# Last quarter of the last MLP product with tokens in the partitions, in a two-layer hybrid decoder

## Chip, cores, metric

The kernel runs on one core of one Trainium2 chip. The metric is the device time of one execution in microseconds (us). The median of several runs is compared; one further execution is recorded by the hardware profiler, and its trace gives the profile.

## What is computed

The reference is a decoder of two layers on x of 512 tokens by 1024 (fp32). Each layer has a mixing part (one projection, window attention, retention, two gated products, an output product) and an MLP; at the end stands one more norm.

```python
def rmsnorm(x, g):
    y = x * rsqrt(mean(x * x, axis=-1) + EPS)
    return y * g

def hybrid_layer(x, ...):
    ...                                   # mixing part: x = x + mixed @ w_out
    h2 = rmsnorm(x, g_mlp)                # (512, 1024)
    x = x + square(relu(h2 @ w_up)) @ w_down   # w_up 1024 x 4096, w_down 4096 x 1024
    return x

for l in range(2):
    x = hybrid_layer(x, ...)
return rmsnorm(x, g_final)
```

The change concerns the last quarter of `@ w_down` in layer 2 (1024 of its 4096 rows), the sum with x, and the final norm with `g_final`.

## The kernel before

**Layout.** Everything is held turned: the model dimension lies in the 128 partitions, as `KD` = 8 chunks, and the 512 tokens lie along the free dimension. `x` is a tile of 128 x 8 x 512. A product for one chunk of 128 output features has the weights as the stationary operand (128 x 128) and the activations as the moving one.

**Three products for one.** Each fp32 factor is kept as a high and a low part in the type fp32r. `products` (L293 to L295) issues three matmuls for each pair: high with high, high with low, low with high, all added up in one bank of PSUM.

**Weights.** They arrive in units of 128 x 1024 numbers (512 KB). `load_until` puts the loads on SP's DMA queue, three units ahead of the splitting; `split_until` makes the high part on ScalarE (L248) and the low part on VectorE (L249). The parts go into three rotating buffers `hi`, `lo`, or, at the very end, into `homes`: tiles of four banks that `slots` hands out (names `r...`), so that they can stay there and be used more than once. `first` shifts the place of some units inside the rotating buffers by `ASIDE` numbers.

**The MLP.** `mlp_sequence` interleaves the two products: pairs of `w_up` chunks (`pair`; the last one is `narrow_pair`, whose products have 256 columns) and, behind each quarter, two chunks at a time of `w_down` (`two_chunks`), added to x by `put_down` (L1146). What comes out of `w_up` is squared, split and kept as `up[q]`, eight pairs of 128 x 512, in `r` tiles or in tiles of the tag `big` (`uhi`, `ulo`; six buffers in all). Layer 2's last quarter is `end(layer, uT)`.

**`end` before.** The 512 tokens are cut into two halves of 256, `Half`. For each half the eight chunks of output features are computed one after the other (the first four side by side in four banks, the rest one by one). `put` adds the bank to x, squares the sum, adds up the squares over the chunks in `acc` and multiplies x by the final gain, which is one column for each chunk. The sum over the partitions is a matmul with ones in fp32 (`sums`, L452). `finish` takes the root, the reciprocal of 128 x 256 numbers (L476), multiplies each chunk (L480) and stores it (L482, L484). `first.finish` runs inside the second half's products, `second.finish` behind the last one. The weights' units stay in place for the second half: the first three in `hi` and `lo`, five in `homes`. The output has the shape (128, 8, 512), and the host turns it.

**PSUM.** `ps_mm` has five banks for products, `ps_aux` three for the rest. The kernel adds products to a bank that ScalarE has written in other places too (`resume`, in `narrow_pair` L1056 and `wide_pair` L1111).

**Order.** The program's text gives the priorities; a scheduler with a timing simulation then fixes each engine's order, and an instruction that is ready may be put ahead of earlier ones that aren't. Each engine works in its order, and a queue's DMAs are issued in theirs.

Of the kernel before, what the change touches and what calls it, by code (L numbers as in the profile page):

```python
# [10 lines left out]
F32 = mybir.dt.float32  # L11
F32R = mybir.dt.float32r
AF = mybir.ActivationFunctionType
ALU = mybir.AluOpType
# [104 lines left out]


@with_exitstack
def decoder(ctx, tc, xT, x_first, w_in, w_a, w_b, w_out, w_up, w_down, tables, decay, band, out):
    nc = tc.nc
    weights = {"w_in": w_in, "w_a": w_a, "w_b": w_b, "w_out": w_out, "w_up": w_up, "w_down": w_down}

# [8 lines left out]
    def f32(ap):  # L134
        return ap.bitcast(F32)

    def temp(name="t"):
        return tmp.tile([P, T], F32, tag="t", name=name)
# [4 lines left out]
    def bank(pool, name):  # L143
        return pool.tile([P, T], F32, tag=pool.name, name=name)
# [1 line left out]

    n_gain, n_sink = (2 * DEPTH + 1) * KD, DEPTH * N_Q
    little_x = const.tile([P, P + KD * T], F32, name="x")  # L150
    gain = little_x[:, P - n_gain : P]
    sink = little_x[:, P - n_gain - n_sink : P - n_gain]
# [71 lines left out]
    def split_until(n):  # L224
        while state["split"] < min(n, len(order)):
            i = state["split"]
            load_until(i + 3)
            paired = order[i][1] == "pair"
            if paired:
                add_part(i)  # L230
            raw = raws[i]
            if homes and i >= len(order) - len(homes):
                home = homes[len(order) - 1 - i]
                hi, lo = (home[:, 2 * a : 2 * a + 2, :].rearrange("p a t -> p (a t)") for a in range(2))
            else:


                first = (ASIDE, ASIDE) if paired or i >= len(order) - 8 else (0, 0)
                if paired and wide(order[i][2]):
                    first = (ASIDE, 0)  # L240
                hi, lo = (
                    wpool.tile([P, UNIT + P], F32R, tag=n, name=n)[:, a : a + UNIT] for n, a in zip(("hi", "lo"), first)
                )
            for at in (LEFT,) if paired and order[i][3] == 3 else halves(i):
                if i == 0 and at.start == 0:
                    nc.vector.tensor_copy(hi[:, at], raw[:, at])
                else:
                    nc.scalar.activation(hi[:, at], raw[:, at], AF.Copy)  # L248
                nc.vector.tensor_tensor(lo[:, at], raw[:, at], f32(hi[:, at]), ALU.subtract)  # L249
            raws.pop(i - 3 if paired else i, None)  # L250
            parts[i] = (hi, lo)
            state["split"] += 1

    def unit(name, layer):
        i = state["next"]
        assert order[i][:2] == (layer, name), (order[i], layer, name)
        state["next"] += 1
        split_until(i + 3)
        return parts.pop(i)
# [27 lines left out]
    def products(ps, pairs, start, stop, resume=False):  # L287


        n = len(pairs)  # L290
        for i, ((ah, al), (bh, bl)) in enumerate(pairs):
            more = {"skip_group_check": True} if resume else {}
            nc.tensor.matmul(ps, ah, bh, start=start and i == 0, stop=False, **more)  # L293
            nc.tensor.matmul(ps, ah, bl, start=False, stop=False, **more)  # L294
            nc.tensor.matmul(ps, al, bh, start=False, stop=stop and i == n - 1, **more)  # L295
# [118 lines left out]


    def end(layer, uT):
        homes.extend(slots.four()[0] for _ in range(5))
        units = []
        H = T // 2
        g_last = 2 * DEPTH * KD  # L420

        def unit_at(i):
            if len(units) == i:
                units.append(unit("w_down", layer))
            return units[i]

        def half_products(ps, i, col, moving, at, start, stop):
            hi, lo = unit_at(i)
            cols = slice(col, col + P)
            products(ps, [((hi[:, cols], lo[:, cols]), tuple(m[:, at] for m in moving))], start, stop)  # L430

        class Half:
            def __init__(self, at):
                self.at = at
                self.acc = tmp.tile([P, T], F32, tag="acc", name="acc", bufs=1)[:, :H]

            def put(self, c, ps):
                xa = x[:, c, self.at]
                nc.vector.tensor_tensor(xa, xa, ps, ALU.add)
                if c == 0:  # L440
                    nc.scalar.activation(self.acc, xa, AF.Square)
                else:
                    sq = temp("sq")[:, :H]
                    nc.scalar.activation(sq, xa, AF.Square)
                    if c < KD - 1:
                        nc.vector.tensor_tensor(self.acc, self.acc, sq, ALU.add)
                    else:
                        self.last = sq
                nc.scalar.activation(xa, xa, AF.Copy, scale=gain[:, g_last + c : g_last + c + 1])

            def sums(self, ps, src, start):
                nc.tensor.matmul(ps, f32(ones), src, start=start, stop=not start)  # L452

            def gemm(self, meanwhile=None):
                banks = [bank(ps_mm, "mm")[:, :H] for _ in range(4)]
                for k in range(KD):
                    for c, ps in enumerate(banks):
                        half_products(ps, k // 2, (k % 2) * T + c * P, uT[k], self.at, k == 0, k == KD - 1)
                    if k == 1 and meanwhile:
                        meanwhile()  # L460
                for c, ps in enumerate(banks):
                    self.put(c, ps)
                for c in range(4, KD):
                    ps = bank(ps_mm, "mm")[:, :H]
                    for k in range(KD):
                        half_products(ps, c, k * P, uT[k], self.at, k == 0, k == KD - 1)
                    if c == KD - 1:
                        self.ssq = bank(ps_aux, "ssq")[:, :H]
                        self.sums(self.ssq, self.acc, True)
                    self.put(c, ps)  # L470

            def finish(self):
                self.sums(self.ssq, self.last, False)
                rstd = tmp.tile([P, T], F32, tag="rstd", name="rstd", bufs=2)[:, :H]
                nc.scalar.activation(rstd, self.ssq, AF.Sqrt, bias=eps, scale=1.0 / D)
                nc.vector.reciprocal(rstd, rstd)  # L476
                for k in range(KD):
                    if k % 2 == 0:
                        o = temp("o").rearrange("p (c t) -> p c t", t=H)
                    nc.vector.tensor_tensor(o[:, k % 2, :], x[:, k, self.at], rstd, ALU.mult)  # L480
                    if k in (0, 1, KD - 2, KD - 1):
                        nc.sync.dma_start(out[:, k, self.at], o[:, k % 2, :])  # L482
                    elif k % 2:
                        nc.sync.dma_start(out[:, k - 1 : k + 1, self.at], o)  # L484

        first = Half(slice(0, H))
        first.gemm()
        second = Half(slice(H, T))
        second.gemm(first.finish)
        second.finish()  # L490


    def layer_body(layer):
# [760 lines left out]
    return units  # L1254


def _down_units(w):
    units = []
    for q in range(4):
        rows = w[q * D : (q + 1) * D]  # L1260
        units += _half_grouped(rows) if q == 3 else _units_twos(rows)
    return units


# [31 lines left out]
def _laid_out(x, g_mix, w_in, sinks, w_a, w_b, w_out, g_mlp, w_up, w_down, g_final):  # L1296
    r = np.arange
    wa_rows = np.concatenate([(4 * g + c) * HEAD_DIM + r(HEAD_DIM) for c in range(4) for g in range(2)])
    rotary, decay, band = _tables()
    gains = np.stack([g for l in range(DEPTH) for g in (g_mix[l], g_mlp[l])] + [g_final])  # L1300
    heads = np.array([4 * g + c for c in range(4) for g in range(2)])
    xT = np.ascontiguousarray(x[0].T.reshape(KD, P, T).transpose(1, 0, 2))
    gains = gains.reshape(-1, P).T
    sinks = np.broadcast_to(sinks[:, heads].reshape(1, -1), (P, DEPTH * N_Q))
    return {
        "xT": xT,
        "x_first": np.concatenate([sinks, gains, xT[:, 0, :]], 1),
        "w_in": _stack(w_in, _w_in_units),
        "w_a": _stack(w_a, lambda w: _units_chunks(w[wa_rows], r(D))),
        "w_b": _stack(w_b, _half_grouped),  # L1310
        "w_out": _stack(w_out, _half_grouped),
        "w_up": _stack(w_up, _up_units),
        "w_down": _stack(w_down, _down_units),
        "tables": rotary,
        "decay": decay,
        "band": band,
    }


# [16 lines left out]
```

## Time and profile before

| | us |
|---|---|
| median of 3 runs | 1500.74 (1500.68 to 1500.89) |
| the profiled execution, its own time | 1500.69 |
| its span in the trace | 1498.8 |
| TensorE busy | 1487.5 |
| VectorE busy | 1066.0 |
| ScalarE busy | 757.9 |

The span reaches from the first to the last instruction in the trace; some 1.9 us of the execution's own time lie around it. In the profile PE is TensorE, PEld its weight loads, DVE is VectorE, ACT is ScalarE, SP is the engine that issues most DMAs (SPq is its queue). A timeline row has the start, the length, the engine, the line, the operation, the result and the operands, and in brackets the idle time before it with what ended it. Matmuls are pipelined: each row's length reaches into the next one. A row of one line or tile gives lengths in ns as least, median and greatest.

### The profile page before, as it was taken

How to read it: one execution, taken by the hardware profiler on the slowest of the kernel's cores; microseconds unless marked ns; L12 is line 12 of the kernel's file. 1: busy time of each engine (PE TensorE's matmuls, PEld its weight loads, DVE VectorE, ACT ScalarE, POOL GpSimd, SP SyncE). 2: the span in 40 equal slices, each digit the busy share in tenths (PEclk: the TensorE clock that was granted, in tenths of full speed). 3: DMA queues.
4: the chain of work that ended last, by engine and by line, in shares of the span. 5: the costliest groups of instructions: out<-in, count | busy, mean ns of one | idle time of the engine just before them, and what ended most of it. 6: DMA issues, size and time to landing. Idle time of an engine off the chain costs nothing.

```text
span 1498.8 us, 19490 instructions
## 1 busy us (share of the span) xinstructions
PE 1487.5 (99%) x7468; PEld 1265.3 (84%) x7468; DVE 1066.0 (71%) x1708; ACT 757.9 (51%) x1207; POOL 2.9 (0%) x13
## 2 busy tenths in 40 slices
PE   9999999999999999999999999999999999999997
PEld 7888888888888888888888888888888888888897
DVE  7877568754697777777678765677448877777774
ACT  6657355632564445544455742555226555454562
POOL 0000000000000000000000000000000000000000
PEclk9999999999999999999999999999999999999999
DMA  6422322244323332324443222222442222343331
GB/s 222 128 91 71 99 84 92 71 126 126 98 73 112 99 111 87 112 85 142 155 132 92 85 85 90 82 90 84 126 124 95 91 93 91 99 127 99 102 110 56
DMA packets 52636, 155.03 MB, mean 103 GB/s; under 512 B 6208, under 2 KB 8384, under 8 KB 52544
## 3 DMA queue, kind: packets, MB, share of 16 engines
q1 hardware_dynamic: 52400, 153.54, 32.5%
q8 instruction: 58, 0.95, 0.3%
q14 instruction: 34, 0.28, 0.1%
q10 hardware_dynamic: 144, 0.26, 0.0%
HBM read 146.96 MB, written 4.19 MB: 101 GB/s over the span
## 4 chain that ended last, share of the span: by engine, by line
PE 99%; ACT 1%; DVE 0%; issue 0%; DVEq 0%
PE mm L293 24%; PE mm L295 24%; PE mm L294 24%; PE mm L1085 9%; PE mm L1086 5%; PE rv L293 2%; PE rv L294 2%; PE rv L295 2%; PE score L664 1%; PE pT L629 1%; PE r L294 1%; PE r L295 1%; PE r L293 1%; PE pv L649 0%; PE pv L650 0%; PE ssq L387 0%
## 5 line engine op out<-in xcount | busy, mean ns | idle before, releaser
L248 ACT ACTIVATE hi<-raw 128x1024 fp32r<-128x1024 f32 (+1 forms) x313 | 315.2, 1013 | 451.7 <-PE mm L294 278.6
L249 DVE TENSOR_TENSOR lo<-raw,hi 128x1024 fp32r<-128x1024 f32 (+1 forms) x314 | 363.8, 1164 | 166.7 <-ACT hi L248 165.6
L294 PE MATMUL mm<-r,hi 128*128 128x512 f32 (+1 forms) x784 | 292.9, 374 | 0.0
L293 PE MATMUL mm<-r,hi 128*128 128x512 f32 (+1 forms) x784 | 291.6, 375 | 1.1 <-ACT mm L1056 1.1
L295 PE MATMUL mm<-r,lo 128*128 128x512 f32 (+1 forms) x784 | 288.4, 374 | 0.0
L293 PE MATMUL mm<-xhl,hi 128*128 128x512 f32 (+1 forms) x744 | 283.1, 383 | 0.0
L294 PE MATMUL mm<-xhl,hi 128*128 128x512 f32 (+1 forms) x744 | 281.8, 381 | 0.0
L295 PE MATMUL mm<-xhl,lo 128*128 128x512 f32 (+1 forms) x744 | 280.8, 381 | 0.0
L293 PEld LDWEIGHTS mm<-r,hi 128*128 128x128 f32 x784 | 146.8, 188 | 27.4 <-ACT mm L1056 1.5
L295 PEld LDWEIGHTS mm<-r,lo 128*128 128x128 f32 x784 | 147.0, 188 | 26.6
L294 PEld LDWEIGHTS mm<-r,hi 128*128 128x128 f32 x784 | 147.2, 188 | 25.4
L293 PEld LDWEIGHTS mm<-xhl,hi 128*128 128x128 f32 x744 | 140.2, 189 | 24.8 <-ACT xhl L303 0.4
L295 PEld LDWEIGHTS mm<-xhl,lo 128*128 128x128 f32 x744 | 139.8, 188 | 25.0
L294 PEld LDWEIGHTS mm<-xhl,hi 128*128 128x128 f32 x744 | 139.9, 188 | 24.5
L1085 PE MATMUL mm<-r,hi 128*128 128x512 f32 x352 | 124.4, 391 | 0.0
L1086 PE MATMUL mm<-r,lo 128*128 128x256 f32 x352 | 97.5, 277 | 0.0
L1085 PE MATMUL mm<-xhl,hi 128*128 128x512 f32 x264 | 93.3, 390 | 0.0
L1085 PEld LDWEIGHTS mm<-r,hi 128*128 128x128 f32 x352 | 66.1, 188 | 14.2 <-ACT mm L1111 0.6
L1086 PE MATMUL mm<-xhl,lo 128*128 128x256 f32 x264 | 73.1, 277 | 0.0
L1086 PEld LDWEIGHTS mm<-r,lo 128*128 128x128 f32 x352 | 66.1, 188 | 1.7
L1146 DVE TENSOR_TENSOR x<-x,mm 128x512 f32<-128x512 f32 x56 | 37.8, 686 | 39.0 <-PE mm L295 39.0
L1085 PEld LDWEIGHTS mm<-xhl,hi 128*128 128x128 f32 x264 | 49.6, 188 | 10.2
(210 smaller groups left out, 2110.5 us busy)
## 6 DMA issues: line engine op xcount, KB each, us to landing
raw<-w_in_in SPq DMA_DIRECT2D x89, 512.0 KB, 3.5
raw<-w_down_in SPq DMA_DIRECT2D x64, 512.0 KB, 3.6
raw<-w_up_in SPq DMA_DIRECT2D x36, 512.0 KB, 3.6
raw<-w_up_in SPq DMA_DIRECT2D x56, 256.0 KB, 2.7
raw<-w_b_in SPq DMA_DIRECT2D x16, 512.0 KB, 3.5
raw<-w_out_in SPq DMA_DIRECT2D x16, 512.0 KB, 3.8
raw<-w_a_in SPq DMA_DIRECT2D x8, 512.0 KB, 3.6
x<-xT_in SPq DMA_DIRECT2D x15, 256.0 KB, 3.9
```

The lines of the kernel that those rows point to most:

```text
L248: nc.scalar.activation(hi[:, at], raw[:, at], AF.Copy)
L249: nc.vector.tensor_tensor(lo[:, at], raw[:, at], f32(hi[:, at]), ALU.subtract)
L293: nc.tensor.matmul(ps, ah, bh, start=start and i == 0, stop=False, **more)
L294: nc.tensor.matmul(ps, ah, bl, start=False, stop=False, **more)
L295: nc.tensor.matmul(ps, al, bh, start=False, stop=stop and i == n - 1, **more)
L629: nc.tensor.transpose(pt[:, i * P : (i + 1) * P], sm[:, at : at + P], ident)
L664: nc.tensor.matmul(ps[:, g * w : (g + 1) * w], q_s[g][:, c, at], part[:, keys], start=i == 0, stop=i == 1)
L1085: nc.tensor.matmul(both, hi[:, c], m, start=start and k == 0, stop=False, **more)
L1086: nc.tensor.matmul(ps[:, :H], lo[:, c], m[:, 0, :], start=False, stop=k == 3 and start, **more)
L1146: nc.vector.tensor_tensor(x[:, c, :], x[:, c, :], ps, ALU.add)
```

## The change

Layer 2's last quarter comes out with tokens in the partitions: the activations `uT` are now the stationary operand (128 features by a block of 128 tokens), the weights the moving one, up to 512 columns wide (half the model dimension). There are four token blocks (`NB`) and two halves `f` of the model dimension.

- For f = 0 the four blocks are computed side by side in four banks. x's chunks are turned by transposes on TensorE (`turned`), copied by ScalarE to `x0`, and VectorE adds the banks to them.
- For f = 1 the blocks come one after the other, the last one in two halves of 256 columns. ScalarE copies the turned x into the bank first (`seeded`), and the products are added to it. The turn of the next step is written ahead of the products of the current one.
- The squares are summed along the free dimension by ScalarE's accumulator, as one column for each block, so that the sum over partitions by matmuls goes. Root and reciprocal have one column. The final gain, now along the free dimension, is loaded as a table of 128 x 1024 (`g_last`, two loads of 256 KB in temporaries).
- The weights' last eight units are laid out by halves of the model dimension on the host; the last four of them are in `homes` (before: five); the units before these lie unshifted in their buffers.
- The output is (512, 1024); each block's two halves are stored apart, the last block's first half from ScalarE's queue.

```diff
-    n_gain, n_sink = (2 * DEPTH + 1) * KD, DEPTH * N_Q
+    n_gain, n_sink = 2 * DEPTH * KD, DEPTH * N_Q
...
-                first = (ASIDE, ASIDE) if paired or i >= len(order) - 8 else (0, 0)
+                first = (ASIDE, ASIDE) if paired else (0, 0)
...
     def end(layer, uT):
-        homes.extend(slots.four()[0] for _ in range(5))
...
+        homes.extend(slots.four()[0] for _ in range(4))
+        gains = [temp("gains") for _ in range(2)]
+        for f in range(2):
+            nc.sync.dma_start(gains[f], g_last[:, f * T : (f + 1) * T])
+        two = [big("x0") for _ in range(2)]
+        x0 = [two[b // 2][:, b % 2, :] for b in range(NB)]
+        sums = [small.tile([P, 8], F32, tag="st", name="st") for _ in range(NB)]
+
+        def turned(f, b, at=slice(0, T)):
+
+            pt = bank(ps_aux, "xT")[:, : at.stop - at.start]
+            for i, c in enumerate(range(at.start // P, at.stop // P)):
+                nc.tensor.transpose(pt[:, i * P : (i + 1) * P], x[:, 4 * f + c, b * P : (b + 1) * P], ident)
+            return pt
+
+        def multiply(ps, k, b, weights, start, stop, resume=False, at=slice(0, T)):
+            hi, lo = weights
+            cols, rows = slice((k % 2) * T + at.start, (k % 2) * T + at.stop), slice(b * P, (b + 1) * P)
+            products(ps, [(tuple(m[:, rows] for m in uT[k]), (hi[:, cols], lo[:, cols]))], start, stop, resume)
+
+
+        for b in range(NB):
+            nc.scalar.activation(x0[b], turned(0, b), AF.Copy)
+        banks = [bank(ps_mm, "mm") for _ in range(NB)]
+        for u in range(4):
+            weights = unit("w_down", layer)
+            split_until(state["next"] + 2 + u)
+            for j in range(2):
+                k = 2 * u + j
+                for b, ps in enumerate(banks):
+                    multiply(ps, k, b, weights, k == 0, k == KD - 1)
+
+
         H = T // 2
...
+        steps = [(b, at) for b in range(NB) for at in ((slice(0, T),) if b < NB - 1 else (slice(0, H), slice(H, T)))]
+
+        def seeded(b, at):
+            ps = bank(ps_mm, "mm")[:, : at.stop - at.start]
+            nc.scalar.activation(ps, turned(1, b, at), AF.Copy)
+            return ps
+
+        units = [unit("w_down", layer) for _ in range(4)]
+        ahead = seeded(*steps[0])
+        for b, ps in enumerate(banks):
+            so_far = sums[b][:, 0:1]
+            nc.vector.tensor_tensor(x0[b], x0[b], ps, ALU.add)
+            nc.scalar.activation(temp("sq"), x0[b], AF.Square, accum_out=so_far)
+            nc.vector.tensor_scalar(so_far, so_far, 1.0 / D, EPS, ALU.mult, ALU.add)
+            nc.vector.tensor_tensor(x0[b], x0[b], gains[0], ALU.mult)
+        for i, (b, at) in enumerate(steps):
+            ps = ahead
+            if i + 1 < len(steps):
+                ahead = seeded(*steps[i + 1])
+            for k in range(KD):
+                multiply(ps, k, b, units[k // 2], False, False, True, at)
+            rows = slice(b * P, (b + 1) * P)
+            so_far, more = sums[b][:, 0:1], sums[b][:, 2:3]
+            nc.scalar.activation(temp("sq")[:, at], ps, AF.Square, accum_out=more)
+            if at.start == 0:
+                o = temp("o")
+            if at.stop < T:
+                nc.vector.tensor_tensor(o[:, at], ps, gains[1][:, at], ALU.mult)
+                nc.vector.scalar_tensor_tensor(so_far, more, 1.0 / D, so_far, ALU.mult, ALU.add)
+                continue
+            nc.scalar.activation(more, more, AF.Sqrt, bias=so_far, scale=1.0 / D)
+            nc.vector.reciprocal(more, more)
+            nc.vector.scalar_tensor_tensor(o[:, at], ps, more, gains[1][:, at], ALU.mult, ALU.mult)
+            if at.start > 0:
+                nc.vector.tensor_scalar(o[:, : at.start], o[:, : at.start], more, None, ALU.mult)
+            nc.scalar.activation(x0[b], x0[b], AF.Copy, scale=more)
+            (nc.scalar if at.start > 0 else nc.sync).dma_start(out[rows, :T], x0[b])
+            nc.sync.dma_start(out[rows, T:], o)
...
-def _down_units(w):
+def _down_units(w, last):
     units = []
     for q in range(4):
         rows = w[q * D : (q + 1) * D]
-        units += _half_grouped(rows) if q == 3 else _units_twos(rows)
+        if q < 3:
+            units += _units_twos(rows)
+        elif last:
+            units += _units_group(rows, np.arange(T)) + _units_group(rows, T + np.arange(T))
+        else:
+            units += _half_grouped(rows)
     return units
...
-    out = nc.dram_tensor("y_out", (P, KD, T), F32, kind="ExternalOutput").ap()
+    out = nc.dram_tensor("y_out", (T, D), F32, kind="ExternalOutput").ap()
...
-    return np.ascontiguousarray(y.transpose(1, 0, 2).reshape(D, T).T)[None]
+    return y[None]
```

More of the change, by code (lines that the diff above doesn't have):

```diff
@@ L121, in decoder @@
 @with_exitstack
-def decoder(ctx, tc, xT, x_first, w_in, w_a, w_b, w_out, w_up, w_down, tables, decay, band, out):
+def decoder(ctx, tc, xT, x_first, w_in, w_a, w_b, w_out, w_up, w_down, tables, decay, band, g_last, out):
     nc = tc.nc
@@ L416, in end @@
     def end(layer, uT):
-        homes.extend(slots.four()[0] for _ in range(5))
-        units = []
-        H = T // 2
[L420 to L490, printed above, removed]
+        homes.extend(slots.four()[0] for _ in range(4))
[5 more added lines that the diff above has]
+        sums = [small.tile([P, 8], F32, tag="st", name="st") for _ in range(NB)]
@@ L1299, in _laid_out @@
     rotary, decay, band = _tables()
-    gains = np.stack([g for l in range(DEPTH) for g in (g_mix[l], g_mlp[l])] + [g_final])
+    gains = np.stack([g for l in range(DEPTH) for g in (g_mix[l], g_mlp[l])])
     heads = np.array([4 * g + c for c in range(4) for g in range(2)])
@@ L1312, in _laid_out @@
         "w_up": _stack(w_up, _up_units),
-        "w_down": _stack(w_down, _down_units),
+        "w_down": np.ascontiguousarray(np.stack([np.stack(_down_units(m, l == DEPTH - 1)) for l, m in enumerate(w_down)])),
         "tables": rotary,
@@ L1316, in _laid_out @@
         "band": band,
+        "g_last": np.ascontiguousarray(np.broadcast_to(g_final, (P, D))),
     }
```

## The prediction

> **What bounds the kernel now.** I read the page first: the busy totals and the chain that ended last.
>
> ```profile
> span 1498.8 us, 19490 instructions
> PE 1487.5 (99%) x7468; PEld 1265.3 (84%) x7468; DVE 1066.0 (71%) x1708; ACT 757.9 (51%) x1207; POOL 2.9 (0%) x13
> ...
> PE 99%; ACT 1%; DVE 0%; issue 0%; DVEq 0%
> ```
>
> TensorE (PE) is busy for 1487.5 of 1498.8 us, and the chain is TensorE for 99%. Only 11.3 us of the span lie outside it. So a change can win in two ways only: by taking time out of TensorE's own stream, or out of those 11.3 us. Nearly all of the latter is the end of the program. The timeline of the last 11 us:
>
> ```profile
> 1488.25 0.28 PE L295 MATMUL mm<-r,r 128*128 128x256 f32 x1
> ...
> 1488.58 0.42 DVE L439 TENSOR_TENSOR x<-x,mm 128x256 f32<-128x256 f32 x1 [1.55 <-PE mm L295]
> 1489.03 0.42 ACT L444 ACTIVATE sq<-x 128x256 f32<-128x256 f32 x1 [1.92 <-DVE x L439]
> ...
> 1490.74 1.75 DVE L476 RECIPROCAL rstd<-rstd 128x256 f32<-128x256 f32 x1 [1.74 <-ACT rstd L475]
> 1492.53 2.77 DVE L480 TENSOR_TENSOR o<-x,rstd 128x256 f32<-128x256 f32 x8
> ...
> 1495.13 0.93 SPq L482 DMA_DIRECT2D y_out<-o  x2
> ```
>
> From the start of the last product (1488.25) to the end of the span (1498.8) it is 10.55 us, a pure chain: add, square, sum over partitions by a product with ones, root, a reciprocal of 256 columns (1.75), eight scalings (2.77), the last store. This is the first place that the change touches. The second is the stage before it, the last quarter of the second MLP product, where TensorE never rests. I take its prices from TensorE's timeline:
>
> ```profile
> 1401.20 0.39 PE L293 MATMUL mm<-r,hi 128*128 128x512 f32 x1
> ...
> 1404.60 0.39 PE L293 MATMUL mm<-r,hi 128*128 128x512 f32 x1
> ...
> 1431.92 0.28 PE L293 MATMUL mm<-xhl,hi 128*128 128x256 f32 x1
> ...
> 1465.70 0.59 PE L452 MATMUL ssq<-acc,ones 128*128 128x256 f32 x2
> ...
> 1466.25 0.28 PE L294 MATMUL mm<-r,hi 128*128 128x256 f32 x1
> ...
> 1480.33 0.28 PE L295 MATMUL mm<-r,r 128*128 128x256 f32 x1
> ```
>
> The second column is the length of one matmul, in which the next one already runs; what counts is start to start. From 1401.20 to 1404.60 there are 15 steps of 512 columns: 0.2267 us each. From 1480.33 to 1488.25 (the first row of the last fence) there are 66 steps of 256 columns whose weights lie in the `r` tiles: 0.120. Two halves cost 0.240 where one whole costs 0.2267. A pair of `ssq` products between them costs 1466.25 - 1465.70 = 0.55 less one ordinary step, 0.43.
>
> **The stage on TensorE, before.** The last pair of the first MLP product issues 7 x 4 x 3 = 84 products of 256 columns from 1431.92; the stage follows without a gap with 8 chunks x 8 k x 3 x 2 halves = 384. From 1431.92 to the last start at 1488.25 that is 467 steps and two `ssq` pairs (the third hides in the final chain): (56.33 - 0.86) / 467 = 0.1188 a step. The stage is 384 x 0.1188 + 0.86 = 46.48 us.
>
> **The stage after.** Four token blocks x two halves of the model dimension x 8 k x 3 = 192 products of 512 columns; the last 24 are cut into 48 of 256. So 168 x 0.2267 = 38.09 and 48 x 0.120 = 5.76. Both `ssq` pairs go. New are 32 transposes of x, in nine turns (seven of four, two of two). The kernel already turns tiles this way:
>
> ```profile
> 779.23 0.60 PE L579 MATMUL vT<-ident,v 128*128 128x128 f32 x4
> ...
> 779.90 0.39 PE L293 MATMUL mm<-xhl,hi 128*128 128x512 f32 x1
> ...
> L629 PE MATMUL pT<-ident,sm x112: 270/272/299, 61.7 to 867.3; 128*128 128x128 f32 x112
> ...
>   ACT r L300: 23.1, 20
> ```
>
> From the first of four to the second product behind them it is 779.90 - 779.23 = 0.67; less one ordinary 0.2267 leaves 0.445 a turn, 0.111 a transpose. 32 x 0.111 = 3.55. Sum: 38.09 + 5.76 + 3.55 = 47.40, so TensorE's stream gets 0.92 us longer: the wider products win 2.0, the dropped sums 0.86, and the transposes take more than both.
>
> One length of 272 ns stands against a step of 111 ns. The Trainium skill (TensorE: Matmul & The Clock Gate, Part 4: PE-mode transpose) gives a transpose in a kernel about 275 ns, most of it access latency. The length agrees with the trace, the step doesn't; charged at that figure, 32 would be 8.8 us by an estimate from the page, and the change would lose. That is a rival below.
>
> **The new waits.** The prices of the new steps, from the same operations elsewhere in the kernel:
>
> ```profile
> L1111 ACT ACTIVATE mm<-mm x22: 578/582/582, 466.6 to 1413.0; 128x512 f32<-128x512 f32 x22
> L684 ACT ACTIVATE sm<-sm,st x64: 383/496/512, 55.2 to 853.8; 128x256 f32<-128x256 f32 x48, 128x128 f32<-128x128 f32 x16
> L684 ACT ACTIVATION_READ_ACCUMULATOR sm<-sm,st x64: 185/187/193, 55.5 to 854.3; 128x1 f32 x64
> L687 ACT ACTIVATE st<-st x32: 186/188/205, 56.0 to 855.3; 128x2 f32<-128x2 f32 x32
> L689 DVE RECIPROCAL st<-st x32: 151/166/168, 56.4 to 857.5; 128x2 f32<-128x2 f32 x32
> L303 ACT ACTIVATE r<-rv,rcol x16: 690/690/695, 167.7 to 987.2; 128x512 fp32r<-128x512 f32 x16
> DMA to landing us min/median/max: 2.0/2.1/2.9
> SPq L1331 <- DMA y_out<-o: 1.7, 1, 1.7
> ```
>
> (The landing line is that of the eight `spill` stores, 256 KB in rows of 2 KB, the form of the new stores; the last line is the wait of the closing instruction for the last store.) Each of the five seeded steps needs a turn, then a ScalarE copy from bank to bank, then its products. For step 0 that is 0.60 (four transposes) + 0.03 + 0.58 + 0.05 = 1.26 us from the end of the first four-bank product. What TensorE can do meanwhile are the turns of steps 1 and 2, which need nothing but x and a free bank of three: three turns are 1.33 us, and the wait vanishes; with only its own turn in hand it is 0.82. I take 0.1, because the order on each engine is made by a scheduler that issues what is ready ahead of what isn't. The later steps have 5.4 us (24 x 0.2267) of products over their seeds. Behind a waiting copy on ScalarE stand only the squares of the same stage.
>
> **The end after.** From the start of the last product: 0.33 to its reader (1488.25 to 1488.58); square with its accumulator read, 0.50 (between 0.42, the square alone, and 0.61, with all of the 0.19 read); root of one column, 0.25 (0.19 by L687, some more for the column as bias); reciprocal of one column, 0.17 in place of 1.75; the product of the last 256 columns 0.42 (as the add at 1488.58) and the scaling of the other 256, 0.35 (2.77 / 8); beside these ScalarE scales the block's first half, 0.69. Four hops at 0.03. Sum 2.14. Then two stores of 256 KB start together on two queues. One alone lands in 2.1. At the rate of the last stores, 348 GB/s at best in the row below, the second 256 KB is 0.75 more if they share the engines: between 2.1 and 2.9, I take 2.8.
>
> ```profile
> GB/s 284 240 150 249 38 199 254 333 257 5 0 11 0 5 0 0 0 0 0 0 0 115 297 156 142 0 0 0 0 0 0 0 0 0 0 35 267 348 49 5
> ```
>
> (The 40 slices of 1440 to 1500 us.) The closing: the wait of 1.7 begins when the last issue ends, at 1496.06, so 1498.8 - 1497.76 = 1.05 follows the last landing. 2.14 + 2.8 + 1.05 = 5.99 against 10.55: 4.56 us won.
>
> **What costs nothing, and its cover.** The first-half x goes out through ScalarE copies and gets its products added on VectorE, its square, its gain: all while the seeded steps run, 22 us of products over some 10 to 12 us of work on either engine (nine copies and nine squares at 0.58 to 0.69, eight or so passes of VectorE like them). The two loads of the final gain (512 KB) enter SP's queue ahead of the last weight loads, and must wait for a free temporary; behind them wait the last four weight units. One unit now lasts 24 x 0.2267 = 5.4 us in place of 24 x 0.1188 = 2.9, so at 250 to 330 GB/s 1.6 to 2.1 us of extra load is covered; without that cover it would be just these. The smaller first table and the other place of four weight units in their buffers: nothing, since 512-column steps cost 0.2267 wherever I looked.
>
> **Sum.** 0.92 + 0.1 - 4.56 = -3.54 against the profiled execution's own 1500.69 us; the median, 1500.74, is 0.05 above it. Forecast 1497.2 us. Bounds: end 4.9 to 6.6 us (0.42 for the square and 2.1 for the stores; 0.61, 2.9, and 0.3 more in the closing), stage +0.65 (last 48 steps at 0.113, 256 columns at the rate of 512) to +1.74 (the 0.82 wait): 1495.7 to 1498.5. A difference of 0.2% is 3.0 us, about what a measurement here can tell: the line is 1497.74, inside this range.
>
> **Rivals.** (a) Turns stand open: TensorE takes its instructions in order, and if each of the nine turns sits right in front of work that needs its copy, each costs up to 0.82 (0.55 for the two short ones): 6.8 us, in place of 0.1. That is +3.2, 1503.9, slower. It decides from about the fifth open turn. Against it: where the kernel turns tiles now, the line `ACT r L300` stands under who waited: ScalarE waits for TensorE, 23.1 us in 20 times, and no idle time of TensorE is listed; for it: the turn of step 0 has no products left in front. 6%. (b) One to three turns open, at step 0 and the cut last block: 0.8 to 2.4 us, 1497.9 to 1499.5. 15%. (c) Transposes charged at their 272 ns: 8.70 for 3.55, 5.15 more, 1502.4. For it: `x` is fp32 and the stage is fuller than attention; against it, the four in 0.445. 5%. This is the reading of the skill's page. (d) The wider product doesn't do what it says: if a 512-column step costs 0.2376, two of 0.1188, because both operands come from the `r` tiles, 168 x 0.0109 = 1.8 us are lost, 1499.0. 5%. The forecast keeps 69%.
>
> **Numbers.** Of the forecast's 69% I give 56 to more than 3.0 us gained (four fifths: its middle is 0.54 beyond the line), 13 to less; (b), (c) and (d) lie within 0.2%; (a) beyond it. Faster 0.56, same 0.38, slower 0.06. Range 1495.8 to 1499.7: forecast, (b) and (d), with little left out.
>
> **What would show it.** Right: 512-column products 0.227 apart in the stage; transposes 0.11 apart; no TensorE gap above 0.2 us between the first four-bank product and the end; last product about 1 us later than 1488.25; about 6.0 us from its start to the end of the span. Wrong: idle TensorE in front of L293 put down to a ScalarE copy into `mm`; stores that land later than 3 us; a stage over 48.5 us.

## The result, and the profile after

The changed kernel takes 1497.08 us (median; 1496.85 to 1497.62) against 1500.58 us (1500.21 to 1500.99) of the kernel before beside it: 0.9977 of its time, 95% interval 0.9969 to 0.9986, 3.5 us won. The forecast was 1497.2.

The profiled execution took 1496.93 us of its own time. The page, in its busy totals and its chain:

```profile
span 1495.1 us, 19175 instructions
...
PE 1487.1 (99%) x7324; PEld 1259.6 (84%) x7324; DVE 1055.9 (71%) x1685; ACT 757.1 (51%) x1208; POOL 2.9 (0%) x13
...
PE 99%; ACT 1%; DVE 0%; issue 0%; DVEq 0%; ACTq 0%
```

TensorE is as busy as before (1487.1 for 1487.5 us) and still 99% of the chain; the span is 3.7 us shorter, and what lies outside TensorE fell from 11.3 to 8.0 us. So most of the time went from outside TensorE's stream. The timeline of the end shows where:

```profile
1488.98 0.28 PE L295 MATMUL mm<-r,r 128*128 128x256 f32 x1
1489.35 0.38 ACT L474 ACTIVATE sq<-mm 128x256 f32<-128x256 f32 x1 [2.45 <-PE mm L295]
1489.63 0.20 ACT L474 ACTIVATION_READ_ACCUMULATOR sq<-mm 128x1 f32 x1
1489.86 0.29 ACT L481 ACTIVATE st<-st 128x1 f32<-128x1 f32 x1
1490.18 0.16 DVE L482 RECIPROCAL st<-st 128x1 f32<-128x1 f32 x1 [2.76 <-ACT st L481]
1490.38 0.72 ACT L486 ACTIVATE x<-x,st 128x512 f32<-128x512 f32 x1 [0.23 <-DVE st L482]
1490.38 0.48 DVE L483 SCALAR_TENSOR_TENSOR o<-mm,st,gains 128x256 f32<-128x256 f32 x1
1490.78 0.34 DVE L485 TENSOR_SCALAR o<-o,st 128x256 f32<-128x256 f32 x1
1491.13 0.39 ACTq L487 DMA_DIRECT2D y_out<-x  x1
1491.15 0.33 SPq L488 DMA_DIRECT2D y_out<-o  x1
```

From the start of the last product to the end of the span it is 1495.1 - 1488.98 = 6.12 us, where it was 10.55: 4.43 won. The last product starts 0.73 us later than before (1488.98 for 1488.25). 4.43 - 0.73 is the 3.70 of the span. In the old chain the reciprocal of 256 columns (1.75) and the eight scalings (2.77) stood; here stand 0.16 and, side by side, 0.72 and 0.48 + 0.34. The add (0.42) and the sum over the partitions by products (0.70, at 1489.50) are gone as well; the last store, on the other side, takes 3.0 to its landing for 2.1.

The 0.73 holds some chance. TensorE's products come in the same order in all twelve profiled executions of this document up to 1378 us, just ahead of the first transpose. Of one of the last of them, first the row before, then the row after:

```profile
1376.06 0.39 PE L1085 MATMUL mm<-r,hi 128*128 128x512 f32 x1
...
1375.65 0.39 PE L1083 MATMUL mm<-r,hi 128*128 128x512 f32 x1
```

This one product starts 0.41 us earlier in the profile after, where TensorE's work is still the same; over the twelve executions it starts anywhere between 1375.45 and 1376.16, and at 1376.03 in the changed kernel without its turns, told below. Counted from it, the last product starts after 113.33 us in place of 112.19: the stage is 1.14 longer, the parts make 4.43 - 1.14 = 3.29, and 0.41 of the span's 3.70 is a difference of executions. Below, "from the common product" means from this one.

The rows of TensorE and ScalarE around the turns, from the timeline:

```profile
1378.22 0.49 PE L429 MATMUL xT<-ident,x 128*128 128x128 f32 x3
...
1378.78 0.39 PE L294 MATMUL mm<-r,hi 128*128 128x512 f32 x1
...
1394.31 0.49 PE L429 MATMUL xT<-ident,x 128*128 128x128 f32 x3
...
1433.02 0.28 PE L293 MATMUL mm<-xhl,hi 128*128 128x256 f32 x1
...
1442.20 1.04 PE L429 MATMUL xT<-ident,x 128*128 128x128 f32 x8
...
1449.57 0.58 ACT L455 ACTIVATE mm<-xT 128x512 f32<-128x512 f32 x1
...
1465.59 0.60 PE L429 MATMUL xT<-ident,x 128*128 128x128 f32 x4
1465.94 0.48 PE L293 MATMUL mm<-r,r 128*128 128x512 f32 x1
1466.26 0.40 PE L294 MATMUL mm<-r,r 128*128 128x512 f32 x1
1466.46 0.58 ACT L455 ACTIVATE mm<-xT 128x512 f32<-128x512 f32 x1
```

L429 is the transposes, L455 the seeds. Twelve of the 32 transposes, in four groups of three, one for each free bank, run between 1378 and 1395, inside pairs of the first MLP product, 47 to 63 us ahead of the first four-bank product (1441.50). Eight run at 1442.2, those of step 0 among them, so that its seed is copied at 1449.57, in the middle of the first four-bank product. Step 1's turn stands between that product and step 0's first product (1465.59), and its copy runs beside step 0. What TensorE waited for, over the whole span:

```profile
PE mm L293 <- ACT mm L1054: 1.1, 2, 0.6
PE warm L273 <- DVE ones L268: 1.1, 1, 1.1
```

Columns: waiter, releaser, us in total, times, longest. No seed is among them (the copy of L1054 is that of `narrow_pair`, and the kernel before waits 1.1 us for it too).

The group of the tile `xT`, the closing waits of SP's queue, and the stores by the DMA issues (KB each, median us to landing) from 1440 us on:

```profile
L429 PE MATMUL xT<-ident,x x32: 269/272/275, 1378.2 to 1483.2; 128*128 128x128 f32 x32
...
SPq L1335 <- DMA y_out<-o: 2.2, 1, 2.2
SPq L1335 <- DMA y_out<-x: 0.3, 1, 0.3
...
y_out<-o SPq DMA_DIRECT2D x4, 256.0 KB, 2.4
y_out<-x SPq DMA_DIRECT2D x3, 256.0 KB, 2.0
y_out<-x ACTq DMA_DIRECT2D x1, 256.0 KB, 3.0
```

A transpose is 272 ns long. The last block's first half, alone on ScalarE's queue but issued together with the second half, lands in 3.0 us; the three first halves before it, each issued about 0.4 us ahead of its second half, take 2.0.

### The profile page after: what moved, and what is told of

It reads as the page before. It is cut to its first block, busy times and chain, and to the rows that moved or that the text cites. A ratio compares the mean times of both kernels' runs of the same rounds, so it can differ in the third digit from the quotient of the medians.

```text
span 1495.1 us, 19175 instructions
## 1 busy us (share of the span) xinstructions
PE 1487.1 (99%) x7324; PEld 1259.6 (84%) x7324; DVE 1055.9 (71%) x1685; ACT 757.1 (51%) x1208; POOL 2.9 (0%) x13
## 4 chain that ended last, share of the span: by engine, by line
PE 99%; ACT 1%; DVE 0%; issue 0%; DVEq 0%; ACTq 0%
PE mm L293 24%; PE mm L295 24%; PE mm L294 24%; PE mm L1083 9%; PE mm L1084 5%; PE rv L293 2%; PE rv L294 2%; PE rv L295 2%; PE score L662 1%; PE pT L627 1%; PE r L294 1%; PE r L295 1%; PE r L293 1%; PE pv L647 0%; PE pv L648 0%; PE ssq L387 0%
## 5 line engine op out<-in xcount | busy, mean ns | idle before, releaser
L294 PE MATMUL mm<-r,hi 128*128 128x512 f32 (+1 forms) x768 | 288.9, 376 | 0.0
L293 PE MATMUL mm<-r,hi 128*128 128x512 f32 (+1 forms) x768 | 287.5, 377 | 1.1 <-ACT mm L1054 1.1
L295 PE MATMUL mm<-r,lo 128*128 128x512 f32 (+1 forms) x768 | 284.8, 376 | 0.0
L294 PE MATMUL mm<-xhl,hi 128*128 128x512 f32 (+1 forms) x744 | 282.1, 381 | 0.0
L293 PEld LDWEIGHTS mm<-r,hi 128*128 128x128 f32 x768 | 143.9, 188 | 27.2 <-ACT mm L1054 1.5
L294 PEld LDWEIGHTS mm<-r,hi 128*128 128x128 f32 x768 | 144.3, 188 | 25.3
L294 PEld LDWEIGHTS mm<-xhl,hi 128*128 128x128 f32 x744 | 140.0, 188 | 24.4
L1083 PEld LDWEIGHTS mm<-r,hi 128*128 128x128 f32 x352 | 66.1, 188 | 14.1 <-ACT mm L1109 0.6
```

What stands on the lines that cost most here:

```text
L1083: nc.tensor.matmul(both, hi[:, c], m, start=start and k == 0, stop=False, **more)
```

## The experiments

Theory: TensorE's stream pays about 0.11 us for each transpose and wins by the wider product; no turn is waited for, because turns are issued early; the end is shorter because the norm has one column. Rivals: a transpose costs its length; turns stand open; the wider product, the cut of the last block or the second queue does something else than thought. Each run is told against the kernel before on the same chip, 1500.47 to 1500.78 us in the three groups.

**The price of a transpose.** Each issued twice:

```diff
-                nc.tensor.transpose(pt[...], x[...], ident)
+                for _ in range(2):
+                    nc.tensor.transpose(pt[...], x[...], ident)
```

> Each transpose is issued twice, 64 in place of 32. If a transpose costs TensorE its step of 0.110 us, the time grows by 3.5 us, to about 1500.6. If it costs its length of 0.272 us, it grows by 8.7 us, to 1505.8. If ScalarE's copies were what mattered, it wouldn't grow, since their number is unchanged.

It took 1500.48 us (0.9999, 0.9989 to 1.0008), a span of 1498.4. Timeline and group of the tile:

```profile
L430 PE MATMUL xT<-ident,x x64: 270/272/273, 1378.1 to 1486.5; 128*128 128x128 f32 x64
...
1467.37 2.12 PE L430 MATMUL xT<-ident,x 128*128 128x128 f32 x18
1469.25 0.48 PE L293 MATMUL mm<-r,r 128*128 128x512 f32 x1
...
1492.24 0.28 PE L295 MATMUL mm<-r,r 128*128 128x256 f32 x1
```

The last product starts 1492.24 - 1488.98 = 3.26 us later (3.34 from the common product): 0.10 for each of 32 more, although each row is 272 ns long. Eighteen in a row take 1469.25 - 1467.37 = 1.88, 0.104 each.

The other direction, with no turning at all (the copies take x as it lies):

```diff
-            nc.scalar.activation(x0[b], turned(0, b), AF.Copy)
+            nc.scalar.activation(x0[b], x[:, b, :], AF.Copy)
...
-            nc.scalar.activation(ps, turned(1, b, at), AF.Copy)
+            nc.scalar.activation(ps, x[:, 4 + b, at], AF.Copy)
```

> The turning of x is left out: the copies take x as it lies, so the sum with x is of other numbers. All other instructions stay. If the transposes cost 0.111 us each, 3.5 us faster: 1493.6; if they cost their length, 8.7 us: 1488.4. With their copies hidden, no more than this can be had by turning x in another way.

1493.39 us (0.9950, 0.9935 to 0.9965). The last product in its timeline:

```profile
1485.51 0.28 PE L295 MATMUL mm<-r,r 128*128 128x256 f32 x1
```

3.47 us earlier than in the changed kernel, and 3.85 from the common product: 0.12 a transpose. That is a little more than 0.10 because with a whole turn a slow product goes too: behind a turn a product of 512 columns takes 0.32 us to the next start (1465.94 to 1466.26) in place of 0.227. Both directions agree to this; the length as price is out.

**Turns that stand open.** Each seeded step's turn is held until the last product of the step before has been issued:

```diff
-        ahead = seeded(*steps[0])
...
-            ps = ahead
-            if i + 1 < len(steps):
-                ahead = seeded(*steps[i + 1])
+            with tc.issue_after(done.ins):
+                ps = seeded(b, at)
             for k in range(KD):
-                multiply(ps, k, b, units[k // 2], False, False, True, at)
+                done = multiply(ps, k, b, units[k // 2], False, False, True, at)
```

> The turn of each seeded step is held back behind the last product of the step before it, so that its copy has no products to hide behind. If an open turn costs what the prediction said (0.82 us for four transposes, 0.55 for two), three full ones and two short ones add 3.6 us: 1500.7, with idle time of TensorE ahead of the products that ends with a ScalarE copy into the bank. If TensorE finds other work, or the copy is quicker than the products behind it need, nothing is added.

1502.38 us (1.0013, 1.0003 to 1.0022): above the kernel before. First the waits, then the timeline at one of the five steps:

```profile
PE mm L293 <- ACT mm L456: 4.1, 5, 0.9
...
1472.20 0.60 PE L430 MATMUL xT<-ident,x 128*128 128x128 f32 x4
1472.46 0.60 ACT L473 ACTIVATE sq<-mm 128x512 f32<-128x512 f32 x1 [5.11 <-PE mm L295]
...
1473.05 0.59 ACT L456 ACTIVATE mm<-xT 128x512 f32<-128x512 f32 x1
1473.69 0.50 PE L293 MATMUL mm<-r,r 128*128 128x512 f32 x1 [0.89 <-ACT mm L456]
```

Now TensorE waits five times for the seed, 4.1 us listed; its span is 1500.5 for 1495.1, 5.4 more. That is 1.08 a turn in the mean of three turns of four transposes and two of two, where the prediction had 0.82 and 0.55. At the step shown two things are added. The copy doesn't start when the transposes end (1472.80) but 0.25 later (1473.05), because ScalarE is still in the square of the step before, which became ready during the turn (1472.46). And the first product behind the stop takes 0.34 to the next start (1474.03) in place of 0.227. With both, the 0.82 become 1.18; from the turn's start to the second product it is 1474.03 - 1472.20 = 1.83, less 0.227 and the 0.445 of a covered turn, 1.16. So the early turns carry the win: with these five open the change would have lost.

**The wider product.** The 72 products of 512 columns of the seeded steps as 144 of 256:

```diff
-                multiply(ps, k, b, units[k // 2], False, False, True, at)
+                for part in range(at.start, at.stop, H):
+                    multiply(ps[:, part - at.start : part - at.start + H], k, b, units[k // 2], False, False, True, slice(part, part + H))
```

> The 72 products of 512 columns in the seeded steps are issued as 144 of 256. If the wider product was worth 2 x 0.120 - 0.2267 = 0.013 us, this adds 1.0 us: 1498.0, all of it on TensorE ahead of the last product. If width makes no difference, nothing is added; if operands that both lie in the r tiles already slowed the wide products, less is added than 1.0.

1497.91 us (0.9984, 0.9975 to 0.9994), 0.83 over the changed kernel in medians, 0.9 in span (1496.0). From its timeline:

```profile
1469.80 0.28 PE L294 MATMUL mm<-r,uhi 128*128 128x256 f32 x1
...
1470.88 0.28 PE L294 MATMUL mm<-r,r 128*128 128x256 f32 x1
```

Nine steps in 1.08, 0.120 each; 72 x (0.240 - 0.2267) = 0.96 was due. The last product starts at 1489.85, 0.87 later, and 0.79 from the common product.

The wider product without turning anything: the kernel before, with its 512 tokens in one piece.

```diff
-        H = T // 2
+        H = T
...
-                        o = temp("o").rearrange("p (c t) -> p c t", t=H)
+                        o = big("o")
...
-        first = Half(slice(0, H))
...
+        whole = Half(slice(0, T))
+        whole.gemm()
+        whole.finish()
```

> The kernel before, with the 512 tokens not cut in halves: wide products in the old layout. The stage on TensorE should take 192 x 0.2267 = 43.5 us in place of 46.5, and the chain behind the last product about 15.1 us in place of 10.55 (reciprocal 3.35 for 1.75, eight scalings some 5.0 for 2.8): together 1.5 us slower than before, 1502.2. If the gain of the change came from the width alone, this one would be as fast as the changed kernel.

1502.70 us (1.0014, 1.0005 to 1.0023), slower. Its end in the timeline:

```profile
1485.17 0.39 PE L295 MATMUL mm<-r,r 128*128 128x512 f32 x1
...
1488.88 3.35 DVE L476 RECIPROCAL rstd<-rstd 128x512 f32<-128x512 f32 x1 [2.60 <-ACT rstd L475]
1492.27 4.91 DVE L480 TENSOR_TENSOR o<-x,rstd 128x512 f32<-128x512 f32 x8
...
1496.60 1.12 SPq L482 DMA_DIRECT2D y_out<-o  x2
```

The stage ends 3.08 us earlier than before (1488.25; from the common product 2.99, where 3.0 was expected), and all of it and more is lost behind it: the span ends at 1501.0, 15.83 us after the last product's start. In the old layout a wider product makes the end longer by more than it wins; in the changed one it doesn't, and transposes are the price.

**The end: the cut and the second queue.** Last block uncut, so one turn of four and one square of 512 columns:

```diff
-        steps = [(b, at) for b in range(NB) for at in ((slice(0, T),) if b < NB - 1 else (slice(0, H), slice(H, T)))]
+        steps = [(b, at) for b in range(NB) for at in (slice(0, T),)]
...
-            (nc.scalar if at.start > 0 else nc.sync).dma_start(out[rows, :T], x0[b])
+            (nc.scalar if b == NB - 1 else nc.sync).dma_start(out[rows, :T], x0[b])
```

> The last token block is not cut in two halves of 256 columns. TensorE should win 24 x 0.013 = 0.3 us; the end loses some 0.25 us because the last square has 512 columns, and the scaling is one pass of 512 in place of two of 256, about the same. No difference that can be measured: 1496.9 to 1497.3. If the cut is what makes the end short, it would be 0.5 us or more slower.

1496.71 us (0.9974, 0.9963 to 0.9984), a little below what was expected; span 1495.3, end 6.22. In time that can't be told from the changed kernel. In the trace the last product starts 112.92 us from the common product in place of 113.33, 0.4 won where 0.3 was expected, and the end is 0.1 longer: the cut isn't what makes the end short, and nothing shows that it pays.

Last store of the first half on SP's queue too:

```diff
-            (nc.scalar if at.start > 0 else nc.sync).dma_start(out[rows, :T], x0[b])
+            nc.sync.dma_start(out[rows, :T], x0[b])
```

> The last block's first half is stored from SP's queue like the rest, not from ScalarE's. If both queues share the same DMA engines, only the second issue comes later, by 0.35 us at most: 1497.1 to 1497.4. If a second queue gave bandwidth of its own, 0.75 us would be lost: 1497.8.

1497.46 us (0.9979, 0.9970 to 0.9988). The last product and the two stores in its timeline:

```profile
1489.04 0.28 PE L295 MATMUL mm<-r,r 128*128 128x256 f32 x1
...
1491.19 0.33 SPq L487 DMA_DIRECT2D y_out<-x  x1
1491.61 0.39 SPq L488 DMA_DIRECT2D y_out<-o  x1
```

The time lies between the two that were expected, so the trace decides. The last product comes 113.33 us from the common product, as in the changed kernel. The end is 1495.5 - 1489.04 = 6.46, 0.34 more, and the second issue is 0.42 behind the first. In the changed kernel the two stores land 3.0 and 2.6 us after their issues; with a bandwidth of its own for each queue both should have landed in about the 2.0 of the earlier first halves. The second queue saves an issue, not a transfer.

**Turning off TensorE.** TensorE's stream still bounds the kernel, and 3.5 us of it are transposes. VectorE turns blocks of 32 x 32, and 32 DMAs of 64 KB put the blocks in their places in x's own memory:

```diff
+        x0, x1 = ([x[:, 4 * f + b, :] for b in range(NB)] for f in range(2))
+        for f in range(2):
+            blocks = [...]
+            for c in range(4):
...
+                for q in range(4):
...
+                    nc.vector.transpose(to[:, :, c, :], src[:, :, q, :])
+            for q in range(4):
...
+                for r in range(4):
...
+                    nc.sync.dma_start(to[:, :, r, :], src)
...
-            nc.scalar.activation(x0[b], turned(0, b), AF.Copy)
...
-            nc.scalar.activation(ps, turned(1, b, at), AF.Copy)
+            nc.scalar.activation(ps, x1[b][:, at], AF.Copy)
```

> The changed kernel with x turned by VectorE (blocks of 32 x 32) and by DMAs that put the blocks in place, in place of the 32 transposes on TensorE. If the transposes cost 3.55 us and the DMAs (32 of 64 KB in pieces of 128 B) are through before the first block's sums and the first seed are wanted, 22 us after the stage begins: 3.5 us faster, 1493.6. If the DMAs are late, TensorE waits ahead of the first seeded step, and each us of it takes one of the 3.5 back.

1494.35 us (1494.25 to 1494.72; 0.9958, 0.9941 to 0.9974), the fastest version with the two below: 2.7 us under the changed kernel in medians, and clear of the two runs of the end above, which shared its chip (1496.37 at the lowest). The rows of its 32 block transposes (the second half of the model dimension goes through `blocks`, the first through the tiles of `x0`, which the trace names `x`), its DMA issues, TensorE's waits, and the two rows behind these:

```profile
L429 DVE STREAM_TRANSPOSE blocks<-x x16: 267/270/303, 1435.0 to 1445.1; 128x128 f32<-128x128 f32 x16
L429 DVE STREAM_TRANSPOSE x<-x x16: 268/270/311, 1440.6 to 1453.1; 128x128 f32<-128x128 f32 x16
...
x<-blocks SPq DMA_DIRECT2D x16, 64.0 KB, 2.3
x<-x SPq DMA_DIRECT2D x16, 64.0 KB, 3.0
...
PE mm L293 <- ACT hi L248: 0.6, 1, 0.6
PE mm L293 <- ACT mm L465: 0.2, 1, 0.2
...
1438.56 0.72 PE L293 MATMUL mm<-hi,r 128*128 128x512 f32 x2 [0.56 <-ACT hi L248]
...
1468.64 0.50 PE L293 MATMUL mm<-r,r 128*128 128x512 f32 x1 [0.19 <-ACT mm L465]
```

VectorE pays 32 x 0.27 us beside TensorE's work. The version won 0.75 us less than expected, and TensorE has two waits in the stage, 0.8 together, that the changed kernel hasn't: for a split of weights, and for a seed. The last product starts at 1486.65, 1.14 later than with no turning, and 1.32 from the common product. The two stops make up that much: from start to start the steps that end in them take 0.84 (from 1437.72) and 0.57 (from 1468.07) where 0.12 and 0.227 are usual, and the first step behind each takes 0.1 more.

The larger wait looks like one of order. TensorE's queue has the first products of the four-bank product ahead of the last products of the narrow pair, and they wait for ScalarE's split, which starts at 1437.44, released by a product of TensorE (L294) and not by a load. With no turning the same products come later in the queue, at 1440.37, and nothing waits. In front of the smaller one stands VectorE's add of the first half, which frees the bank and waits 3.8 us for the DMAs of `x<-x`.

Two attempts at those 0.8 us. The last block uncut as well:

> The turn by VectorE and DMAs together with the uncut last block. Each alone was faster than the changed kernel, by 2.7 and 0.4 us; they touch different places (the stream of TensorE before the last block, and the last block), so the sum is expected: 1494.0. If the cut also hid something that the DMAs now need, less.

1494.37 us (0.9957, 0.9940 to 0.9973): nothing won. And, on top of that, every second DMA of the first half from ScalarE's queue:

```diff
-                    nc.sync.dma_start(to[:, :, r, :], src)
+                    (nc.scalar if f == 0 and r % 2 else nc.sync).dma_start(to[:, :, r, :], src)
```

> As dma_uncut, but half of the DMAs that place the first half of x are issued from ScalarE's queue. In dma_turn TensorE waited 0.6 us ahead of the second seeded step because its bank came free only after those DMAs had landed. If SP's issues are what makes them late, this wait goes: 1493.6. If the DMA engines are (pieces of 128 B), or if the issues delay ScalarE's splits, nothing is won: 1494.0 or more.

1494.76 us (0.9958, 0.9944 to 0.9973). The expectation took the two waits for each other: the seed's is the 0.2, and the 0.6 is the split's. The wait for the seed left the list, and from the common product the last one starts 110.16 us later in place of 110.46; but its end is 0.2 longer, and the time didn't fall. The 0.6 for the split stays in all three versions (0.56 each), as an order of the scheduler's would. Whether another order would win it back was not tried.

## Why the prediction was right

**The stage, +0.92 + 0.1; measured +0.73, and +1.14 from the common product.** The terms held. From the first product of the narrow pair (1433.02) to the last start (1488.98) are 55.96 us with 20 transposes in them; by the prediction's terms it is 84 x 0.1188 + 47.40 - 12 x 0.111 - 0.12 (the last step lies behind its own start) = 55.93. The transposes' 0.111 lies between the 0.104 and 0.120 of the two runs, and the wider product was worth 0.8 to 0.9 us when it was taken away (0.96 by the steps). The twelve early transposes cost what the others do where they stand: 1378.78 - 1378.22 - 0.2267 = 0.33 for three. But the narrow pair starts 1.51 later from the common product, where twelve are 1.33; the other 0.18 lie in the pairs between and were not followed. So the stage was 0.2 dearer than its 0.92, without the 0.1 for the seed. By the parts of the traces the change wins 3.29 us; that the 3.50 of the medians stands nearer to the forecast's 3.54 is luck as far as the traces show. One side figure of the prediction enters nothing and doesn't come out of its terms: the wider products win 384 x 0.1188 - 43.85 = 1.77, not 2.0. Two of its bounds are off by 0.1 or less: the stage's lower one is +0.60 for +0.65, the end's upper one 6.5 for 6.6.

**The seed of step 0, 0.1; measured none. This step failed in its reason.** The prediction let the turns of steps 1 and 2 fill TensorE while step 0's seed was copied, behind the four-bank product. In fact step 0's turn ran at 1442.2 and its seed at 1449.57, before that product's middle: it needs only x and the fifth bank of `ps_mm`, both free by then, and a scheduler that issues what is ready doesn't keep it for later. The prediction named that rule and didn't apply it to the turns themselves. Only step 1's turn stands at 1465.59.

**The price of an open turn, 0.82; measured 1.16 (1.08 in the mean of the five).** The working counted the copy as soon as the transposes end and the products behind it at their full pace. On ScalarE the square of the step before is ready first and holds the copy for 0.25 us (1472.80 to 1473.05), and the first step behind the stop is 0.11 longer. Rival (a), slower by open turns, and (b), a few of them open, were therefore real in their mechanism and cheaper on paper than on the chip: five open turns already give 1502.38, and the 3.5 us won are used up by 3.5 / 1.08, between the third and the fourth, where the prediction put the point of decision at about the fifth. What spoke against both was the order, which left no turn open, not the price.

**The end, 5.99; measured 6.12.** To the stores' issue 2.15 us (2.14 by the sum; hop 0.37 for 0.33, square and accumulator 0.48 for 0.50, root 0.29 for 0.25, reciprocal 0.16 for 0.17). Landing 3.0 for 2.8. Behind the landing (1491.13 + 3.0 = 1494.13) the closing 0.97 for 1.05.

**The rivals of size.** (c) is out: with 32 more transposes at 272 ns the time would have grown by 8.7 us, not 3.3. The Trainium skill (TensorE: Matmul & The Clock Gate, Part 4: PE-mode transpose) gives about 275 ns in a kernel; the trace agrees with that as a length and not as a price in a full stream. (d) is out: steps of 512 columns with both operands in `r` tiles come 0.23 apart, and halving them lost time.

**The cover that cost nothing.** TensorE's list of waits shows neither a weight split nor a bank in the stage, so the gain's loads and the first half's way out stayed hidden, as forecast.

## What to carry to other kernels

Price an instruction in a full stream by the step from start to start, and let the doubled instruction confirm it: here 272 ns of length were 0.10 to 0.12 us of time. Before two traces are compared to tenths of a us, find an instruction ahead of the change that both have: here executions lay up to 0.7 us apart at one, and counted from it, versions with the same products agreed to 0.01. Before counting a new wait, ask what its producer needs; if that has long been ready and a bank is free, the order will bring it forward, and if it is held back, count what else becomes ready on the copying engine meanwhile. When a layout is changed for a short end, the work that the new layout adds can be moved once more, to engines that aren't the bound: here VectorE and DMA took the turning and 2.7 us more were won.

## What the hardware showed beside

Two stores of 256 KB from two queues landed no sooner than from one, apart from the issue: 0.34 us less in the end. The Trainium skill (Trainium Kernel Development and Optimization, Key Constraints) says that the queues share 16 DMA engines and that a second one only saves issue time; these runs agree. For a transpose of 128 x 128 another page of the Trainium skill (VectorE: DVE Perf Modes, Rules for kernel authors) points to TensorE where the result may lie in PSUM. The measurement decides otherwise where TensorE is busy for 99% of the span: 32 transposes of 0.27 us on VectorE and 32 small DMAs, longer by any sum of their own, were cheaper than 32 x 0.11 us on TensorE.
